# A hybrid SSM, RG-LRU, retention and RWKV-7 block: the order of issue of all engines taken from a list schedule of its own

## The chip, the cores and the metric

One Trainium2 chip, one of its cores. The metric is the device time of one execution in microseconds, the median of the runs. Engines: PE (TensorE, matmuls), PEld (its weight loads), DVE (VectorE), ACT (ScalarE), POOL (GpSimd), SP (SyncE, which issues most DMAs).

## What is computed

One layer over 512 tokens of width 1024, in float32. The normed input goes through one projection; four token mixers run in parallel on its parts; their outputs are projected, gated and summed; a convolutional feed-forward follows. Cut to its frame:

```python
def hybrid_mixer(h, w_in, ssm_p, lru_p, ret_p, rwkv_p, w_branch, w_out, cos, sin):
...
    proj = h @ w_in
...
    y_ssd = mamba2_branch(m_z, m_xbc, m_dt, *ssm_p)
    y_lru = rglru_branch(l_gate, l_x, *lru_p)
    y_ret = retention_branch(r_q, r_k, r_v, r_g, *ret_p, cos, sin)
    y_rwkv = rwkv7_branch(rw, *rwkv_p)
    ys = jnp.stack([y_ssd, y_lru, y_ret, y_rwkv], axis=2)
    branch = jnp.einsum('bsmw,mwd->bsmd', ys, w_branch)
    gates = jax.nn.sigmoid(gate_logits.astype(F32)).reshape(b, s, N_BRANCH, D_MODEL)
    merged = jnp.sum(gates * branch.astype(F32), axis=2).astype(h.dtype)
    return merged @ w_out
...
    u = causal_dwconv(h @ w_up, conv_w, conv_b)
    val, gt = jnp.split(u, 2, axis=-1)
    return (jax.nn.silu(gt) * val) @ w_down
...
        x = x + hybrid_mixer(h, w_in[l], ssm_p, lru_p, ret_p, rwkv_p, w_branch[l], w_out[l], cos, sin)
        h = rms_norm(x, norm_ffn[l])
        x = x + conv_ffn(h, ffn_up[l], ffn_conv_w[l], ffn_conv_b[l], ffn_down[l])
    return rms_norm(x, norm_final)
```

## The kernel before

Every projection works on tiles of 128 features by 512 tokens. A float32 product is made of three fp32r matmuls: `split` writes a rounded copy on ACT (L100: `whi`, `hh`, `yh`, `gh`) and the rest on DVE (L101: `wlo`, `hl`, ...), and `mm3` (L118) multiplies high by high, low by high and high by low into one of three PSUM tiles `acc` (L119, L120, L121). Weights come in blocks of 512 KB into `raw` (four buffers, `wraw`, L106). `proj_tokens` does the same with tokens on the partitions (L240 to L242), `tail_product` for the out and down products (L955 to L957). In this text a "product" is one such fp32r matmul.

The RWKV-7 mixer is a loop over eight pairs of heads (j = 0 to 7). `rwkv_a1` projects r, k and v and makes the decays; `rwkv_a2` makes the matrices of each chunk of 64 tokens (L372 on PE into `ra`), sends the 32x32 triangles through DRAM and solves them with 62 small DVE instructions (L426, L428); `rwkv_b` joins the inverses with 32 matmuls of 32x32 tiles (16 in L454, 16 in L464, into `rb`), copies on ACT between them (L458, L467), then goes through the eight chunks in sequence: L477 (PE), L479 (DVE), L481 (PE), L482 and L483 (ACT, DVE), L485 (PE), L488 (DVE). These matmuls, those of the other mixers (`inn`: L584, L664, L671, L673, L768, L798, L802, L812) and the transposes (L96) are in plain fp32 and short.

Between the parts of each j, `fill` (L914) takes steps of a generator: the lru tiles (`lru_tiles`: L585 sigmoid, L588 tanh, L591 exp, L598 sqrt, L602 gelu on ACT, each with a table of its own or shared), `ret_pair` and `mamba_group`, then `branch`, which projects the mixers' outputs and gates. After the eight pairs come the last branch, the out product, the up projection with its convolution (L1008, L1010) and the down product.

This is the order in which the code is recorded. The order in which each engine issues is made afterwards by the layer that records the program: it sorts the instructions of all engines by the recorded place and by a cost table that belongs to it, within the dependencies and the buffers. The code intervenes once: `with tc.issue_after(normed)` (L858) puts the setups of the lru and mamba mixers behind the last instruction of the norm. An engine takes its instructions in the order that was made, and waits where one isn't ready.

Of the kernel before, what the change touches and what calls it, by code (L numbers as in the profile page):

```python
# [9 lines left out]
F32R = mybir.dt.float32r  # L10
# [5 lines left out]
P = 128  # L16
# [29 lines left out]
for _key in ([("lora", 0), ("lora", 1)]  # L46
# [11 lines left out]
             + [("down", _j) for _j in range(22)]):  # L58
    _BLK[_key] = len(_BLK)
NBLK = len(_BLK)  # L60


@with_exitstack
def tile_hybrid_block(ctx, tc, x, wts, wzdt, lora, lruw, cpack, consts, rettab, nfin, out):
    nc = tc.nc
# [13 lines left out]
    def cols(name):  # L79
        o, n = _OFF[name]  # L80
        return cp[:, o:o + n]
# [7 lines left out]
    def cdram(name):  # L89
        o, n = _COFF[name]  # L90
        return consts[:, o:o + n]
# [54 lines left out]
    def rms_half(pool, psum, src, u, wname, hh, hl):  # L146

        ts = [src(2 * u + n) for n in range(2)]
        ss = pool.tile([P, 2], F32, name="nss", bufs=2)
        for n, t in enumerate(ts):  # L150
            sq = pool.tile([P, D], F32, name="nsq", bufs=1)
            nc.scalar.activation(out=sq, in_=t, func=AF.Square, accum_out=ss[:, n:n + 1])
        r = rsqrt_small(pool, ss, 1.0 / D, EPS, [P, 2], "nrs")
        xn = []
        for n, t in enumerate(ts):
            y = pool.tile([P, D], F32, name="nxn%d" % n, bufs=2)
            nc.vector.tensor_scalar(out=y, in0=t, scalar1=r[:, n:n + 1], scalar2=None, op0=ALU.mult)
            xn.append(y)
        w = slice(256 * u, 256 * u + 256)
        for ko in range(KT):  # L160
            ps = psum(ko)
            for n in range(2):
                transpose(ps[:, n * P:(n + 1) * P], xn[n][:, ko * P:(ko + 1) * P])
            nc.scalar.activation(out=hh[:, ko, w], in_=ps[:, 0:256], func=AF.Copy, scale=col(wname, ko))
            last = nc.vector.scalar_tensor_tensor(out=hl[:, ko, w], in0=ps[:, 0:256], scalar=col(wname, ko),
                                                  in1=hh[:, ko, w].bitcast(F32), op0=ALU.mult, op1=ALU.subtract)
        return last.ins
# [18 lines left out]
    acc = pss.enter_context(tc.tile_pool(name="acc", bufs=3, space=bass.MemoryType.PSUM))  # L186
    inn = pss.enter_context(tc.tile_pool(name="inn", bufs=1, space=bass.MemoryType.PSUM))
    rps = ExitStack()
    ra = rps.enter_context(tc.tile_pool(name="ra", bufs=2, space=bass.MemoryType.PSUM))
    rb = rps.enter_context(tc.tile_pool(name="rb", bufs=2, space=bass.MemoryType.PSUM))  # L190
    with tc.tile_pool(name="n1", bufs=1) as n1:
        xt, lw = [], []
        for i in range(NT):
            t = n1.tile([P, D], F32, name="x", bufs=4)
# [9 lines left out]
        for u in range(2):  # L204
            normed = rms_half(n1, lambda ko: pools[ko % 3].tile([P, S], F32, name=names[ko % 3]), lambda i: xt[i], u,
                              "norm_mix", hh, hl)
# [318 lines left out]
    def sm(shape):  # L525
        return fl.tile(shape, F32, name="sm", bufs=10)

    def bg(shape):
        return fl.tile(shape, F32, name="bg", bufs=6)
# [33 lines left out]
    def lru_setup():  # L563
        sp = softplus(fl, cols("lru_lam"), [P, 8], "lsp", neg=True)
        c8 = fl.tile([P, 8], F32, name="c8")
        nc.vector.tensor_scalar(out=c8, in0=sp, scalar1=8.0, scalar2=None, op0=ALU.mult)
        m8 = fl.tile([P, 8], F32, name="m8")
        nc.vector.tensor_scalar(out=m8, in0=sp, scalar1=-8.0, scalar2=None, op0=ALU.mult)
        return c8, m8
# [128 lines left out]
    def mamba_setup():  # L698
        z = fl.tile([P, NT, 16], F32, name="dtz")
        zt = bg([P, NT, 256])  # L700

        def put(i, ps):
            nc.vector.tensor_tensor(out=z[:, i, :], in0=ps[:, 256:272], in1=cols("dt_bias"), op=ALU.add)
            nc.scalar.activation(out=zt[:, i, :], in_=ps[:, 0:256], func=AF.Silu)
        proj_tokens("zdt", 0, put)
        dt = softplus(fl, z, [P, NT, 16], "dts")
        na = fl.tile([P, 16], F32, name="na")
        nc.scalar.activation(out=na, in_=cols("a_log"), func=AF.Exp)
        da = fl.tile([P, NT, 16], F32, name="da")
        nc.vector.scalar_tensor_tensor(out=da, in0=dt, scalar=-1.0, in1=na.unsqueeze(1).broadcast_to([P, NT, 16]),  # L710
                                       op0=ALU.mult, op1=ALU.mult)
        ps = inn.tile([P, S], F32, name="inn")
        daf = da.rearrange("p i h -> p (i h)")
        uo = sm([P, 2, P])
        for n, name in enumerate(("upper", "ones")):
            nc.sync.dma_start(out=uo[:, n], in_=cdram(name))
            nc.tensor.matmul(ps[:, n * 64:(n + 1) * 64], uo[:, n], daf, start=True, stop=True)
        ac = fl.tile([P, NT, 16], F32, name="acum")
        nc.vector.tensor_copy(out=ac, in_=ps[:, 0:64].rearrange("p (i h) -> p i h", h=16))
        cd = fl.tile([P, NT, 16], F32, name="cdec")  # L720
        nc.vector.tensor_copy(out=cd, in_=ps[:, 64:128].rearrange("p (i h) -> p i h", h=16))
        de = fl.tile([P, NT, 16], F32, name="dend")
        nc.vector.tensor_tensor(out=de, in0=cd, in1=ac, op=ALU.subtract)
        nc.scalar.activation(out=de, in_=de, func=AF.Exp)
        nc.scalar.activation(out=cd, in_=cd, func=AF.Exp)
        ea = fl.tile([P, NT, 16], F32, name="eac")
        nc.scalar.activation(out=ea, in_=ac, func=AF.Exp)
        ps = inn.tile([P, S], F32, name="inn")
        for i in range(NT):
            transpose(ps[0:16, i * P:(i + 1) * P], ac[:, i, :])  # L730
        at = sm([16, S])
        nc.scalar.copy(out=at, in_=ps[0:16])
        ad = dr.tile([16, S], F32, name="acd")
        nc.sync.dma_start(out=ad, in_=at)
        nac = fl.tile([P, NT, 16], F32, name="nac")
        nc.vector.tensor_scalar(out=nac, in0=ac, scalar1=-1.0, scalar2=None, op0=ALU.mult)
        cap = fl.tile([P, P], F32, name="cap")
        nc.sync.dma_start(out=cap, in_=cdram("cap"))
        return dt, nac, cd, de, ea, ad, cap, zt
# [115 lines left out]
    rope = []  # L855
    omu, hka, hwa, ones2r = rwkv_setup()
    lora_x = rwkv_lora()
    with tc.issue_after(normed):  # L858
        lru_c = lru_setup()
        mam = mamba_setup()  # L860
    msq = fl.tile([P, NT, 4], F32, name="msq")
    ym = dr.tile([NT, 4, P, 256], F32, name="ym")
    brs, mps = ExitStack(), ExitStack()
# [55 lines left out]
    for j in range(8):  # L919
        held = rwkv_a2(j, prep)  # L920
# [10 lines left out]
    tacc = pss.enter_context(tc.tile_pool(name="tacc", bufs=4, space=bass.MemoryType.PSUM))  # L931
# [54 lines left out]
    with ExitStack() as ff:  # L986
        with ExitStack() as up:
# [7 lines left out]
            for f in range(NFF):  # L995
                cv2 = []
                for n, j in enumerate((f, NFF + f)):
                    if first:
                        ps = first.pop(0)
                    else:  # L1000
                        wh, wl = wblock("up", j)
                        ps = tacc.tile([P, S], F32, name="acc")
                        for ko in range(KT):
                            s = slice(ko * P, (ko + 1) * P)
                            mm3(ps, wh[:, s], wl[:, s], hh[:, ko, :], hl[:, ko, :], ko == 0, ko == KT - 1)
                    t = cpool.tile([P, S], F32, name="fc%d" % n, bufs=2)
                    o = j * 3
# [9 lines left out]
        with ExitStack() as dn:  # L1017
# [5 lines left out]
            for dh in range(2):  # L1023
# [18 lines left out]
                    nc.scalar.dma_start(out=out[i * P:(i + 1) * P, S:], in_=ot[:, S:])  # L1042
                tail_product("down", NFF // 2, dh, gh, gl, add_y)
    pss.close()

# [44 lines left out]
def _layout(inputs):  # L1092
# [5 lines left out]
    m_z, m_xbc, m_dt, l_g, l_x, r_q, r_k, r_v, r_g, rw, gates = [int(v) for v in starts]  # L1098
    blocks = np.empty((NBLK, P, 1024), np.float32)

# [81 lines left out]
```

## Time and profile before

| | |
|---|---|
| median of 3 runs | 1602.02 us (1601.81 to 1602.98) |
| the profiled execution: its time, its span | 1603.08 us, 1601.3 us |
| PE busy | 1550.0 us (97%), 8324 matmul records |
| DVE, ACT, POOL busy | 1069.7 (67%), 722.5 (45%), 58.9 (4%) |
| chain that ended last | PE 75%, DVE 16%, ACT 5%, issue 3% |
| HBM traffic | 104 GB/s over the span |

PE's records are modelled at their ends and overlap, so what PE does is read from the starts. A 128x512 product is recorded with 0.39 us, while the next one starts earlier. Idle time of an engine in the listing by group stands behind the last bar, with the releaser.

### The profile page before, as it was taken

To read this page: it belongs to the slowest core of one execution; us is meant where nothing else is said; L and a number is where in the kernel's file an instruction comes from. 1 tells how busy PE (TensorE), PEld (TensorE's weight loads), DVE (VectorE), ACT (ScalarE), POOL (GpSimd) and SP (SyncE) were. 2 spreads that over 40 slices of the span, in tenths; PEclk is the share of its full clock that TensorE was granted. 3 is DMA by queue.
4 is the path that set the end of the run, shared out by engine and by line. 5 is a ranking of instruction groups with operands and counts; after the bars stand their busy time and mean duration, and the time that the engine had idled before them with its cause. 6 is when DMAs were issued, how large, how long until landed. Compare 5 with 4: busy or idle time off the path is not lost.

```text
span 1601.3 us, 22110 instructions
## 1 busy us (share of the span) xinstructions
PE 1550.0 (97%) x8324; PEld 1290.0 (81%) x8324; DVE 1069.7 (67%) x2334; ACT 722.5 (45%) x1190; POOL 58.9 (4%) x78
## 2 busy tenths in 40 slices
PE   7999989999999999999999999999999999999998
PEld 7788767877888788877788788888888888888886
DVE  6797788886887887897656857644436656555233
ACT  6463375535753576358323432323324444444123
POOL 1000000000000000000000100000000000000000
PEclk9999999999999999999999999999999999999999
DMA  5232132333243233443433333343222232233221
GB/s 206 93 125 77 70 115 77 100 107 86 93 126 98 78 112 83 126 132 115 163 105 100 112 104 108 116 151 136 101 79 93 96 104 93 96 101 107 101 96 53
DMA packets 108459, 169.44 MB, mean 106 GB/s; under 512 B 54832, under 2 KB 64304, under 8 KB 108352
## 3 DMA queue, kind: packets, MB, share of 16 engines
q1 hardware_dynamic: 107632, 166.92, 32.6%
q8 instruction: 65, 1.06, 0.3%
q10 hardware_dynamic: 720, 1.11, 0.2%
q14 instruction: 42, 0.34, 0.1%
HBM read 150.66 MB, written 15.24 MB: 104 GB/s over the span
## 4 chain that ended last, share of the span: by engine, by line
PE 75%; DVE 16%; ACT 5%; issue 3%; DMA 1%; SPq 0%; DVEq 0%; ACTq 0%
PE acc L119 16%; PE acc L120 16%; PE acc L121 16%; PE acc L955 3%; PE acc L957 3%; PE acc L956 3%; DVE wlo L101 2%; PE acc L240 2%; PE acc L242 2%; PE acc L241 2%; PE rb L477 2%; DVE prod L426 1%; DVE xr L428 1%; PE ra L372 1%; PE rb L485 1%
## 5 line engine op out<-in xcount | busy, mean ns | idle before, releaser
L119 PE MATMUL acc<-hh,whi 128*128 128x512 f32 (+1 forms) x1240 | 487.1, 393 | 7.1 <-ACT sm L602 4.7
L120 PE MATMUL acc<-hh,wlo 128*128 128x512 f32 (+1 forms) x1240 | 486.3, 392 | 1.0 <-DVE wlo L101 1.0
L121 PE MATMUL acc<-hl,whi 128*128 128x512 f32 (+1 forms) x1240 | 486.7, 393 | 0.0
L101 DVE TENSOR_TENSOR wlo<-raw,whi 128x1024 fp32r<-128x1024 f32 x228 | 279.1, 1225 | 163.2 <-ACT whi L100 162.4
L100 ACT CAST whi<-raw 128x1024 fp32r<-128x1024 f32 x228 | 237.9, 1045 | 214.7 <-PE acc L957 86.5
L119 PEld LDWEIGHTS acc<-hh,whi 128*128 128x128 f32 x1240 | 235.1, 190 | 51.5 <-ACT sm L602 5.4
L120 PEld LDWEIGHTS acc<-hh,wlo 128*128 128x128 f32 x1240 | 234.8, 189 | 44.4 <-DVE wlo L101 1.6
L121 PEld LDWEIGHTS acc<-hl,whi 128*128 128x128 f32 x1240 | 235.0, 190 | 43.5 <-issue 1.9
L1010 DVE SCALAR_TENSOR_TENSOR fc<-acc,fw,fc 128x511 f32<-128x511 f32 x88 | 65.9, 749 | 76.5 <-ACT fc L1008 74.9
L119 PE MATMUL acc<-yh,whi 128*128 128x512 f32 x256 | 101.7, 397 | 1.1 <-ACT yh L100 1.1
L121 PE MATMUL acc<-yl,whi 128*128 128x512 f32 x256 | 101.2, 395 | 0.2 <-DVE yl L101 0.2
L120 PE MATMUL acc<-yh,wlo 128*128 128x512 f32 x256 | 100.6, 393 | 0.0
L1008 ACT ACTIVATE fc<-acc,fw 128x512 f32<-128x512 f32 x44 | 34.3, 779 | 93.8 <-PE acc L121 93.8
L240 PE MATMUL acc<-whi,hh 128*128 128x256 f32 (+1 forms) x256 | 75.7, 296 | 0.4 <-ACT whi L100 0.4
L241 PE MATMUL acc<-wlo,hh 128*128 128x256 f32 (+1 forms) x256 | 74.2, 290 | 0.0
L242 PE MATMUL acc<-whi,hl 128*128 128x256 f32 (+1 forms) x256 | 74.1, 290 | 0.0
L955 PE MATMUL acc<-whi,gh 128*128 128x512 f32 x176 | 69.4, 395 | 0.0
L957 PE MATMUL acc<-whi,gl 128*128 128x512 f32 x176 | 69.4, 395 | 0.0
L956 PE MATMUL acc<-wlo,gh 128*128 128x512 f32 x176 | 69.4, 395 | 0.0
L884 ACT ACTIVATE gt<-acc 128x512 f32<-128x512 f32 x32 | 19.1, 598 | 88.1 <-PE acc L121 83.7
L426 DVE TENSOR_TENSOR prod<-nt,xr 128x60 f32<-128x60 f32 (+24 forms) x248 | 54.0, 218 | 5.2
L428 DVE TENSOR_TENSOR xr<-xr,prod 128x60 f32<-128x60 f32 (+24 forms) x248 | 53.8, 217 | 5.4
(331 smaller groups left out, 2369.1 us busy)
## 6 DMA issues: line engine op xcount, KB each, us to landing
raw<-in_wts_dram SPq DMA_DIRECT2D x226, 512.0 KB, 3.2
yr<-y SPq DMA_DIRECT2D x32, 256.0 KB, 3.0
y<-sm SPq DMA_DIRECT2D x24, 256.0 KB, 2.1
nt<-nd SPq DMA_DIRECT2D x32, 128.0 KB, 2.7
sm<-acd SPq DMA_DIRECT2D x16, 256.0 KB, 3.8
x<-in_x_dram SPq DMA_DIRECT2D x4, 512.0 KB, 5.3
sm<-sm SPq DMA_DIRECT2D x32, 64.0 KB, 2.0
ym<-bg SPq DMA_DIRECT2D x16, 128.0 KB, 1.7
```

The costliest lines, as they stand in the source:

```text
L100: nc.scalar.copy(out=hi, in_=src)
L101: nc.vector.tensor_tensor(out=lo, in0=src, in1=hi.bitcast(F32), op=ALU.subtract)
L119: nc.tensor.matmul(ps, wh, xh, start=first, stop=False)
L120: nc.tensor.matmul(ps, wl, xh, start=False, stop=False)
L121: nc.tensor.matmul(ps, wh, xl, start=False, stop=last)
L240: nc.tensor.matmul(o, hh[:, ko, t], wh[:, s], start=ko == 0, stop=False)
L241: nc.tensor.matmul(o, hh[:, ko, t], wl[:, s], start=False, stop=False)
L242: nc.tensor.matmul(o, hl[:, ko, t], wh[:, s], start=False, stop=ko == KT - 1)
L426: nc.vector.tensor_tensor(out=pr[:, 0:n, 0:m], in0=nt[:, jj, jj + 1:32].unsqueeze(2).broadcast_to([P, n, m]), in1=xr[:, jj:jj + 1, 0:m].br ...
L955: nc.tensor.matmul(ps[i], xh[:, ko, t], w[0][:, s], start=ko == 0, stop=False)
L956: nc.tensor.matmul(ps[i], xh[:, ko, t], w[1][:, s], start=False, stop=False)
L957: nc.tensor.matmul(ps[i], xl[:, ko, t], w[0][:, s], start=False, stop=ko == 2 * nblk - 1)
```

## The change

No instruction of the computation is touched. A function `_order` runs after the whole kernel is recorded. It works out what each instruction depends on by the overlap of what it reads and writes (for PSUM by the whole tile), what buffers it needs, and what it takes (`_cost`). Then it plans: the engine that is free first takes, among its ready instructions, the one recorded first; on PE, matmuls into `acc` come after all others, and any other matmul is left aside while its estimated start lies less than 150 ns back. At the end every instruction is tied behind the one planned before it on its engine, so that the layer's own sorting has no choice left. The one `issue_after` goes. All lines move by 261: L454 is L715 after, L464 is L725, L477 is L738, L119 to L121 are L380 to L382, L602 is L863.

```diff
+_MARGIN = 150.0
+_HOP = 60.0
...
+def _region(ap):
...
+    if t.space == bass.MemoryType.PSUM:
+        return 0, P, 1
...
+def _cost(i):
...
+    if kind == "InstMatmult":
+        mov, sta = i.ins[0].bass_ap, i.ins[1].bass_ap
+        if _base(out.tensor.name) == "acc" or mov.dtype == F32R:
+            return 13.5 + n / 2.4, 170.0
+        if i.is_transpose:
+            return 109.0, 170.0
+        if mov.shape[0] <= 32:
+            return 40.0, 170.0
+        return 2 * max(107.0, n / 1.2 + 2.5), 170.0
+    if kind == "InstDMACopy":
+        return 450.0, 0.0
...
+    return 158.0 + n * 1.04, _HOP
...
+def _order(tc, nc):
...
+                for o, w, q0, q1, b in lst:
+                    if (write or w or bank) and o != k and q0 < p1 and p0 < q1 and b & m:
+                        preds[k].add(o)
...
+        short[k] = i.engine == E.PE and o != "acc"
+        rank[k] = 1 if i.engine == E.PE and o == "acc" else 0
...
+        early = []
+        while ready[e] and short[ready[e][0][1]] and est[ready[e][0][1]] + _MARGIN > t:
+            early.append(heapq.heappop(ready[e]))
+        if early and not ready[e]:
+            heapq.heapify(early)
+            ready[e], early = early, []
+        k = heapq.heappop(ready[e])[1]
+        for x in early:
+            heapq.heappush(ready[e], x)
...
+            est[s] = max(est[s], t if k in after[s] else t + dur if ins[s].engine == e and e != E.SP else done[k])
...
+    for seq in order.values():
+        for a, b in zip(seq, seq[1:]):
+            tc.add_manual_dep(ins[b], ins[a].name, behind, reason="order of issue")
...
-    with tc.issue_after(normed):
-        lru_c = lru_setup()
-        mam = mamba_setup()
+    lru_c = lru_setup()
+    mam = mamba_setup()
...
+    _order(tc, nc)
```

PE at the first matmuls that join the inverses (`xr`, `ab`) for j = 1, before: one matmul, three products, the other fifteen in one piece.

```order
L119 MATMUL acc<-hh,whi 128x512
L454 MATMUL rb<-xr,ab 32x32
L120 MATMUL acc<-hh,wlo 128x512
L121 MATMUL acc<-hl,whi 128x512
L119 MATMUL acc<-hh,whi 128x512
L454 MATMUL rb<-xr,ab 32x32 x15
L120 MATMUL acc<-hh,wlo 128x512
```

After, at the same place, they alternate with the products one by one, up to the sixteenth.

```order
L380 MATMUL acc<-hh,whi 128x512
L715 MATMUL rb<-xr,ab 32x32
L381 MATMUL acc<-hh,wlo 128x512
L715 MATMUL rb<-xr,ab 32x32
L382 MATMUL acc<-hl,whi 128x512
L715 MATMUL rb<-xr,ab 32x32
L380 MATMUL acc<-hh,whi 128x512
L715 MATMUL rb<-xr,ab 32x32
```

Each of L454's matmuls (L715 now) has a product on either side. The second group (`tt`, `xr`) with the first matmuls of the chunks (`sv`, `g`), before: one of the sixteen, two of L477, products, then fifteen.

```order
L464 MATMUL rb<-tt,xr 32x32
L477 MATMUL rb<-sv,g 128x64 x2
L120 MATMUL acc<-hh,wlo 128x512
L121 MATMUL acc<-hl,whi 128x512
L119 MATMUL acc<-hh,whi 128x512
L120 MATMUL acc<-hh,wlo 128x512
L121 MATMUL acc<-hl,whi 128x512
L464 MATMUL rb<-tt,xr 32x32 x15
```

After, L464 (L725) and L477 (L738) stand between each other and between single products.

```order
L725 MATMUL rb<-tt,xr 32x32
L380 MATMUL acc<-hh,whi 128x512
L725 MATMUL rb<-tt,xr 32x32
L738 MATMUL rb<-sv,g 128x64
L725 MATMUL rb<-tt,xr 32x32
L381 MATMUL acc<-hh,wlo 128x512
L725 MATMUL rb<-tt,xr 32x32
L738 MATMUL rb<-sv,g 128x64
L725 MATMUL rb<-tt,xr 32x32
L382 MATMUL acc<-hl,whi 128x512
```

No piece is left there. ACT at the gelus of the first two lru tiles (`sm` from `acc`), before: a table load ahead of the sqrt, the exp and the gelu in turn.

```order
L598 ACT_TABLE_LOAD
L598 ACTIVATE sm<-sm 128x512
L591 ACT_TABLE_LOAD
L591 ACTIVATE sm<-sm,m_440 128x512
L602 ACT_TABLE_LOAD
L602 ACTIVATE sm<-acc 128x512
L593 ACTIVATE sm<-sm 128x512
L100 CAST lh_2399<-cs 128x256
L263 ACTIVATE pr<-acc,omu 128x512
L100 CAST whi<-raw 128x1024
L598 ACT_TABLE_LOAD
L598 ACTIVATE sm<-sm 128x512
```

After, the two sqrts stand together and so do the gelus, with one load each.

```order
L849 ACTIVATE sm<-sm,c_438 128x512
L852 ACT_TABLE_LOAD
L852 ACTIVATE sm<-sm,m_440 128x512
L854 ACTIVATE sm<-sm 128x512
L859 ACT_TABLE_LOAD
L859 ACTIVATE sm<-sm 128x512 x2
L524 ACTIVATE pr<-acc,omu 128x512
L863 ACT_TABLE_LOAD
L863 ACTIVATE sm<-acc 128x512
L361 CAST whi<-raw 128x1024
L863 ACTIVATE sm<-acc 128x512
```

The order after reaches the first gelu without an exp and its table between.

## Rows read from the trace of the kernel before

**Rows 1.** The page's first part: busy time, share of the span, instructions.

```profile
PE 1550.0 (97%) x8324; PEld 1290.0 (81%) x8324; DVE 1069.7 (67%) x2334; ACT 722.5 (45%) x1190; POOL 58.9 (4%) x78
```

**Rows 2.** PE's timeline, three stretches: start, busy us, line, tile, shape, count, idle before.

```profile
10.06 0.48 PE L96 MATMUL inn<-ident,nxn 128*128 128x128 f32 x1 [10.06 <-DVE nxn L157]
...
18.92 0.28 PE L119 MATMUL acc<-hh,whi 128*128 128x256 f32 x1
...
19.88 0.28 PE L121 MATMUL acc<-hl,whi 128*128 128x256 f32 x1
...
1592.32 0.40 PE L957 MATMUL acc<-whi,gl 128*128 128x512 f32 x1
...
1594.42 0.40 PE L957 MATMUL acc<-whi,gl 128*128 128x512 f32 x1
```

**Rows 3.** PE's timeline around L454 for j = 1.

```profile
254.85 0.39 PE L119 MATMUL acc<-hh,whi 128*128 128x512 f32 x1
...
255.53 0.39 PE L119 MATMUL acc<-hh,whi 128*128 128x512 f32 x1
255.85 0.28 PE L454 MATMUL rb<-xr,ab 32*32 32x32 f32 x2
...
256.39 0.39 PE L121 MATMUL acc<-hl,whi 128*128 128x512 f32 x1
256.62 0.40 PE L119 MATMUL acc<-hh,whi 128*128 128x512 f32 x1
256.95 1.09 PE L454 MATMUL rb<-xr,ab 32*32 32x32 f32 x30
...
258.30 0.39 PE L121 MATMUL acc<-hl,whi 128*128 128x512 f32 x1
```

**Rows 4.** Groups by shape, PE: count | busy us, mean ns | idle before, releaser.

```profile
L119 PE MATMUL acc<-hh,whi 128*128 128x512 f32 x1160 | 463.9, 400 | 7.1 <-ACT sm L602 4.7 <-ACT sm L689 2.4
...
L955 PE MATMUL acc<-whi,gh 128*128 128x512 f32 x176 | 69.4, 395 | 0.0
...
L240 PE MATMUL acc<-whi,hh 128*128 128x256 f32 x224 | 66.4, 297 | 0.0
```

**Rows 5.** PE's timeline at 128-row fp32 matmuls, alternating and in a piece.

```profile
161.00 0.40 PE L121 MATMUL acc<-hl,whi 128*128 128x512 f32 x1
161.23 0.33 PE L477 MATMUL rb<-sv,g 128*128 128x64 f32 x2
...
162.15 0.39 PE L121 MATMUL acc<-hl,whi 128*128 128x512 f32 x1
...
339.02 0.39 PE L121 MATMUL acc<-hl,whi 128*128 128x512 f32 x1
339.25 1.05 PE L664 MATMUL inn<-bg,sm 128*128 128x128 f32 x8
...
340.38 0.39 PE L120 MATMUL acc<-hh,wlo 128*128 128x512 f32 x1
```

**Rows 6.** Busy time by stretch: PE, PEld, DVE, ACT, POOL, granted clock, DMA share, GB/s.

```profile
226.40:229.70 3.30, 3.30 (x10) 2.53 (x9) 3.20 (x11) 3.27 (x5) 0.00 (x0) 0.50 0.21 79
```

**Rows 7.** Waits of PE: us in total, times, longest us.

```profile
PE acc L119 <- ACT sm L602: 4.7, 1, 4.7
```

**Rows 8.** PE's timeline around L464 for j = 2.

```profile
374.38 0.24 PE L464 MATMUL rb<-tt,xr 32*32 32x32 f32 x2
374.55 0.50 PE L119 MATMUL acc<-hh,whi 128*128 128x512 f32 x1
374.98 0.69 PE L464 MATMUL rb<-tt,xr 32*32 32x32 f32 x30
375.60 0.66 PE L477 MATMUL rb<-sv,g 128*128 128x64 f32 x4
```

**Rows 9.** Groups by shape, DVE.

```profile
L357 DVE SCALAR_TENSOR_TENSOR bk<-pa,di 64x512 f32<-64x512 f32 x16 | 19.2, 1203 | 3.4 <-ACT di L342 3.3
```

**Rows 10.** Timeline of the weight loads at the lone 32x32 matmul.

```profile
255.85 0.13 PEld L454 LDWEIGHTS rb<-xr,ab 32*32 32x32 f32 x2 [0.35 <-issue]
```

More of the change, by code (lines that the diff above doesn't have):

```diff
@@ L60, with _base, _elems @@
 NBLK = len(_BLK)
+_TABLES = {"Exp": ("exp",), "Tanh": ("exp", "sigmoid", "gelu", "silu"), "Sigmoid": ("sigmoid",), "Sqrt": ("sqrt",),
+           "Gelu_apprx_tanh": ("gelu",), "Silu": ("silu",)}
+_POOL_BUFS = {"acc": 3, "ra": 2, "rb": 2, "tacc": 4}
+_MARGIN = 150.0
+_HOP = 60.0
+def _base(name):
+    return name.rsplit("_", 1)[0]
+def _elems(ap):
+    n = 1
+    for x in ap.shape[1:]:
+        n *= x
+    return n
+_regions = {}
+def _region(ap):
+    t = ap.tensor
+    pitch = 1
+    for n in t.shape[1:]:
+        pitch *= n
+    if t.space == bass.MemoryType.PSUM:
+        return 0, P, 1
+    a = [(int(x[0]), int(x[1])) for x in ap.ap]
+    if t.space == bass.MemoryType.DRAM:
+        p0, n, off, rest = 0, 1, ap.offset, a
+    else:
+        p0, n, off, rest = ap.offset // pitch, a[0][1], ap.offset % pitch, a[1:]
+    key = (off, tuple(x for x in rest if x[0] and x[1] > 1))
+    m = _regions.get(key)
+    if m is None:
+        m = 1
+        for step, count in sorted(key[1]):
+            k = 1
+            while k < count:
+                d = min(k, count - k)
+                m |= m << (step * d)
+                k += d
+        m <<= off
+        _regions[key] = m
+    return p0, p0 + n, m
@@ new lines, in _cost @@
+def _cost(i):
+    E = mybir.EngineType
+    kind = type(i).__name__
+    out = i.outs[0].bass_ap
+    n = _elems(out)
+    if kind == "InstMatmult":
[9 more added lines that the diff above has]
+        return 450.0, 0.0
+    if i.engine == E.Activation:
+        extra = 0.0
+        if kind == "InstActivation":
+            extra = 90.0 * min(2, sum(1 for a in i.ins[1:] if getattr(a, "bass_ap", None) is not None))
+            if len(i.outs) > 1:
+                extra += 200.0
+        return 150.0 + n * 0.877 + extra, _HOP
+    if i.engine == E.Pool:
+        return 250.0 + n * (0.9 if kind == "InstMemset" else 1.0 if kind == "InstTensorCopy" else 2.4), _HOP
+    if getattr(i, "is_tensor_tensor_scan", False):
+        n *= 2
+    if kind == "InstTensorReduce":
+        n = _elems(i.ins[0].bass_ap)
+    return 158.0 + n * 1.04, _HOP
```

151 lines of the change are left out of this document (added).

## Prediction

> **What bounds the kernel now.** I read the busy times first, then the first and the last matmul, then the groups by shape, then single stretches of PE's timeline. PE is busy for 1550.0 us, 97% of the span of 1601.3 [rows 1]; no other engine gets over two thirds. PE's first matmul starts at 10.06; its last starts at 1594.42 and ends near 1594.8 [rows 2]. So of 51.3 us in which PE idles, 10.1 lie ahead of the first matmul and 6.5 behind the last, and 34.7 in between. An order of issue can gain only what PE loses between 10.06 and 1594.42, which are 1584.4 us.
>
> How much is that? I count from below, with distances from start to start, since a matmul's busy time (0.39 us for 128x512) runs past the start of the next. Products of 128x512 start every 0.227 (0.68 for three, 254.85 to 255.53) [rows 3], in the down product every 0.233 (nine from 1592.32 to 1594.42), those of 128x256 every 0.120 (eight from 18.92 to 19.88) [rows 2]. With the counts by shape [rows 4], where the other two lines of each triple have the same count and the branch product adds 3 x 256 and the short halves 3 x 80: 3 x (1160 + 256) x 0.227 = 964; 3 x (176 + 64) x 0.233 = 168; 3 x (224 + 80) x 0.120 = 109; 168 others 31. The fp32 records on 128 rows are 1764: 1684 at 0.112 (eight of L664: 339.02 to 340.38, less two products, are 0.906) [rows 5] and 80 wider ones, 212 together. The 32x32 matmuls take 11.5 where they stand in one piece (below). Sum 1496; PE takes 1584.4, so **88 us are lost**. Of these, 34.7 are recorded idle time; 43 waits cost 0.16 more each, the part of the busy time that runs past the next start (7). Behind the longest waits TensorE's clock was at its lower level of 1.2 GHz, in six stretches of 3.4 to 6.8 us, 30.6 in all; one is 226.4 to 229.7 [rows 6], right behind the wait for L602 [rows 7]. Half the rate there costs some 12. Switches to 32x32 tiles cost 10 and those between other pieces 5 (below). The rest, some 19, is waits too short to be recorded.
>
> **The change part by part.** Instructions stay, but for table loads on ScalarE (66 become 60) and waits on semaphores. What moves is the order, and on PE above all how finely it alternates: over the whole order, the fp32 matmuls stand in 378 pieces between the fp32r products before, and in 847 after. The new code makes them so: a short matmul is taken only if its estimated start lies 150 ns back, and matmuls into one PSUM tile depend on each other, so the second of four becomes ready as the first ends. It is put off, and a long product goes between. The 32x32 matmuls of L454 and L464 (128 each) stand in 30 pieces before and in 236 after, 233 of them single.
>
> *32x32 matmuls, the large term.* One alone: from the product at 255.53 to the second one behind it at 256.39 are 0.86 us; less two products (0.454) it costs 0.406. Fifteen in one piece: 256.62 to 258.30 are 1.68, less 0.454 are 1.226 [rows 3]. From the two lengths a piece costs 0.348 and each matmul in it 0.058. L464: one matmul, one product and the next matmul take 374.38 to 374.98, 0.60; less 0.227 that is 0.373; the piece of fifteen behind it lasts 0.62 to the next matmul [rows 8], so it is 0.032 for each and 0.341 for a piece. The stretch at 374.38, matmul, product, matmul, is already what the new order writes everywhere. Where the neighbours are alike, all 30 pieces show these distances within 0.02 us. 206 more pieces at 0.348: **+71.7 us**, all of it on PE's own path.
>
> *128-row fp32 matmuls.* Their pieces go from some 360 to 681. Two matmuls of L477 that alternate with products cost 161.00 to 162.15 less three products, 0.469, so 0.235 each [rows 5], against 0.224 in one piece. 320 more pieces at 0.012: **+4 us**. Bounds are 0, and 16 if each lost 0.05.
>
> *Waits.* Of the 88 us, 15 are switches; 73 are waits and the slow clock behind them. How many stay can't be read from an order. For their going: 25 of the 34.7 recorded us are short matmuls that stood at PE's head before their operand was there, which is what the 150 ns are meant for; and PE will run behind the plan by those 72 us (the code takes 40 ns for a 32x32 matmul), so other engines are ahead of it. The longest, 4.7 us for L602 on ScalarE [rows 7], came from table loads in a row; the new order loads once for two gelus. Against it: the plan takes 158 + 1.04 n ns on VectorE, 690 for the L357 that feeds L372, and the trace has 1203 [rows 9]; semaphores of the DMA queue aren't in it at all. What is late next is VectorE's chain between L477 and L488 and the split of the weights (L101). Bounds: none stays (-73), all stay (0). I let a third stay, 24, since most of the plan's durations are the trace's and its misses are few: **-49 us**.
>
> *Clock in the alternating pieces.* Sixteen 32x32 matmuls now take about 10 us, in which products fill 0.227 of 0.60. At 1.2 GHz each product could take 0.2 more: 0 to 47 us for 236. No row shows such a stretch of 10 us; the nearest, at 374.38, ran at 2.4 GHz, and the clock fell behind idle time. I take a sixth, **+8 us**.
>
> Start and end: the first ten transposes, the loads of x and the rows behind the last product stand in both orders alike, so 10.1 and 6.5 us stay.
>
> [...] The weight load of the lone 32x32 matmul starts at 255.85, with its matmul, and its loader had idled for 0.35 us [rows 10]. [...]
>
> **Rivals.** (1) *The forecast*: 1603.1 + 71.7 + 4 - 49 + 8 = 1637.8. (2) *The plan doesn't hold on the chip*: it is tighter, every late operand stops PE, and all 73 us of waits stay or come back elsewhere: 1603.1 + 71.7 + 4 + 8 = 1687. L357 speaks for it, PE's lag against it. (3) *The plan holds exactly*: no wait is left, the clock stays up: 1603.1 + 75.7 - 73 = 1606, about no change. (4) *Not slower: the switch of tiles is hidden between products.* Its place is the 233 single matmuls; a separation would cost near 0 in place of 0.348, as if the loader ran ahead: 1637.8 - 71.7 = 1566, faster by 2%. It decides below 0.18 us for each of the 206 (71.7 less the 34.7 by which the forecast is slower, over 206). All 30 pieces and [rows 10] stand against it. (5) *The order isn't what runs*: excluded, as each engine takes the instructions of the built program in turn, and that program has the single matmuls.
>
> **How the numbers follow.** The sum stands against the profiled execution, 1603.08 us; the median of the runs is 1602.02, 1.06 lower, so 1637.8 becomes 1637. Chances: forecast 0.67 (waits and clock between 12 and 57 us in place of 32: 1616 to 1662), plan doesn't hold 0.15 (1662 to 1700), plan exact 0.10 (1600 to 1616, half of it within the bound of no change), hidden switch 0.08. Leaving out the last and most of the second's upper half gives 1608 to 1670. A measurement of this kernel tells about 0.2% from no change, 3.2 us, so slower begins at 1605.2: 0.67 + 0.15 + 0.05 = 0.87; no change 0.05; faster 0.08.
>
> **What would show it.** L715 and L725 (L454 and L464 before) keep their counts, but alternate with products, each product behind one lasting 0.50 and each of them starting 0.32 or more behind its neighbour. PE's busy share stays at 97% or rises while the span grows: the switch hides in busy time. PE's idle time between first and last matmul falls from 34.7 to 10 to 20 us, the 4.7 at the first L863 (L602 before) among what goes. Stretches with nothing but products, behind 1030 us of before, keep their length. Wrong would be the price, if a single 32x32 matmul costs under 0.2 us; the term of the waits, if the idle time stays near 35; the clock term, if 1.2 GHz holds through most of the alternating pieces.

## The result and the profile after

The changed kernel takes 1803.25 us, the median of 4 runs (1794.57 to 1806.22), against 1602.5 of the kernel before on the same chip: 1.125 times as long, with an interval from 1.122 to 1.127. I had forecast slower, but 1637, with 1670 as the upper end. So the sign came out as forecast and the size didn't: +201 us instead of +35.

The page of after, busy time by engine (answers to [rows 1]):

```profile
PE 1715.3 (95%) x8324; PEld 1377.0 (76%) x8324; DVE 1089.8 (60%) x2334; ACT 717.7 (40%) x1184; POOL 58.9 (3%) x78
```

PE has the same number of records and 165 us more busy time. Its idle time grew as well: the span is 1804.2, less 1715.3 that is 88.9; 10.4 lie ahead of the first matmul and 6.5 behind the last, which leaves 72.0 between first and last, where before had 34.7.

The first thing to look at is the granted clock. The core's span and its mean granted clock, before and after:

```profile
core 0: 1601.3 us, clock 0.990
core 0: 1804.2 us, clock 0.913
```

And by stretches of 200 us (columns as in [rows 6]: PE, PEld, DVE, ACT, POOL, granted clock, DMA share, GB/s):

```profile
200.00:400.00 200.00, 180.70 (x952) 143.12 (x951) 148.34 (x354) 90.57 (x161) 11.79 (x16) 0.87 0.26 77
...
1000.00:1200.00 200.00, 196.91 (x871) 144.76 (x871) 100.98 (x231) 54.82 (x91) 6.36 (x8) 0.85 0.25 76
1200.00:1400.00 200.00, 199.17 (x887) 163.96 (x886) 88.27 (x120) 58.34 (x76) 0.00 (x0) 1.00 0.36 123
```

In both traces the granted clock is recorded in stretches, each at 1.00 or at 0.50 (before 14, after 44 of them, the shortest 3.4 us), so a mean of 0.913 means 2 x 0.087 x 1804 = 314 us at 0.50; before, the mean was 0.990, 32 us. No trace shows the clock in GHz: where the prediction and the expectations write 2.4 and 1.2 GHz, the traces show 1.00 and 0.50, and the starts of products an estimated 2.4 and 1.2 columns per ns (at 1.00, 256 more columns take 0.227 less 0.120 us [rows 3] [rows 2]; at 0.50, six products of 512 start in 2.56 us, 226.64 to 229.20 of before). But for 3.4 us at 1434 and the end of the span, the low clock ends near 1175 us, where the last of the eight RWKV blocks ends; the down product runs as before (L1215, L955 before, has a mean of 395 ns in both).

PE's timeline after, at the sixteen matmuls of L715 (L454 before) for j = 7; start, busy us, line, tile, shape (answers to [rows 3]):

```profile
1141.19 0.50 PE L380 MATMUL acc<-yh,whi 128*128 128x512 f32 x1
1141.62 0.28 PE L715 MATMUL rb<-xr,ab 32*32 32x32 f32 x2
1141.83 0.50 PE L381 MATMUL acc<-yh,wlo 128*128 128x512 f32 x1
1142.26 0.28 PE L715 MATMUL rb<-xr,ab 32*32 32x32 f32 x2
...
1144.69 0.80 PE L382 MATMUL acc<-yl,whi 128*128 128x512 f32 x1
1145.42 0.31 PE L715 MATMUL rb<-xr,ab 32*32 32x32 f32 x2
1145.66 0.80 PE L380 MATMUL acc<-yh,whi 128*128 128x512 f32 x1
1146.38 0.31 PE L715 MATMUL rb<-xr,ab 32*32 32x32 f32 x2
```

Read the starts. Up to 1143 one product and one 32x32 matmul take 0.64 us; the forecast had 0.227 + 0.406 = 0.633. From 1144 on the same pair takes 0.96 to 0.97. Between them the clock fell, as busy time and granted clock of the stretches show (j = 7 ahead of the fall and behind it, then j = 6):

```profile
1140.30:1143.80 3.50, 3.50 (x19) 1.79 (x18) 0.00 (x0) 0.00 (x0) 0.00 (x0) 1.00 1.02 281
1143.80:1174.50 30.70, 30.70 (x96) 17.43 (x96) 3.45 (x7) 2.70 (x6) 0.00 (x0) 0.50 0.06 19
997.00:1031.20 34.20, 34.20 (x107) 18.21 (x106) 3.44 (x4) 4.03 (x7) 0.00 (x0) 0.50 0.10 35
```

PE's busy time equals the length of each stretch: no wait is recorded in them, and yet the clock stays at 0.50 for over 30 us, while the 32x32 matmuls come one by one. It recovers soon after they end. The last of j = 6 starts at 1027.85, from 1028.68 products alone start every 0.43 us, from 1031.22 every 0.23:

```profile
1027.85 0.31 PE L725 MATMUL rb<-tt,xr 32*32 32x32 f32 x2
...
1028.68 0.63 PE L381 MATMUL acc<-hh,wlo 128*128 128x512 f32 x1
1029.11 0.63 PE L382 MATMUL acc<-hl,whi 128*128 128x512 f32 x1
...
1031.22 0.39 PE L381 MATMUL acc<-hh,wlo 128*128 128x512 f32 x1
1031.45 0.40 PE L382 MATMUL acc<-hl,whi 128*128 128x512 f32 x1
```

Waits of PE after (us in total, times, longest; answers to [rows 7]):

```profile
PE rb L715 <- DMA xr<-xd: 12.9, 9, 2.8
PE inn L357 <- DVE nxn L418: 10.4, 1, 10.4
PE acc L380 <- DVE prod L687: 7.2, 2, 4.9
PE acc L380 <- ACT sm L863: 6.7, 1, 6.7
PE ra L357 <- DVE bk L642: 6.1, 3, 3.5
```

The second line is the start of the kernel. The wait for the first gelu, 4.7 us before, is 6.7; and the first 32x32 matmul of every block now waits for its DMA.

### The profile page after: what moved, and what is told of

The parts are those of the page before. It is cut to its first block, busy times and chain, and to the rows that moved or that the text cites. A ratio compares the mean times of both kernels' runs of the same rounds, so it can differ in the third digit from the quotient of the medians.

```text
span 1804.2 us, 22101 instructions
## 1 busy us (share of the span) xinstructions
PE 1715.3 (95%) x8324; PEld 1377.0 (76%) x8324; DVE 1089.8 (60%) x2334; ACT 717.7 (40%) x1184; POOL 58.9 (3%) x78
## 4 chain that ended last, share of the span: by engine, by line
PE 75%; DVE 13%; DMA 5%; ACT 3%; issue 2%; SPq 2%; POOL 0%; DVEq 0%; ACTq 0%; POOLq 0%
PE acc L381 16%; PE acc L380 16%; PE acc L382 15%; PE acc L1215 3%; PE acc L1217 3%; PE acc L1216 3%; PE acc L502 2%; PE acc L503 2%; PE acc L501 2%; PE rb L715 2%; PE rb L725 1%; DVE wlo L362 1%; DMA xr<-xd 1%; PE rb L738 1%; DVE sm L820 1%
## 5 line engine op out<-in xcount | busy, mean ns | idle before, releaser
L380 PE MATMUL acc<-hh,whi 128*128 128x512 f32 (+1 forms) x1240 | 514.5, 415 | 19.6 <-DVE prod L687 7.2
L381 PE MATMUL acc<-hh,wlo 128*128 128x512 f32 (+1 forms) x1240 | 514.2, 415 | 4.6 <-DVE wlo L362 4.6
L382 PE MATMUL acc<-hl,whi 128*128 128x512 f32 (+1 forms) x1240 | 513.2, 414 | 0.2
L380 PEld LDWEIGHTS acc<-hh,whi 128*128 128x128 f32 x1240 | 243.2, 196 | 68.8 <-issue 10.1
L381 PEld LDWEIGHTS acc<-hh,wlo 128*128 128x128 f32 x1240 | 243.1, 196 | 51.8 <-DVE wlo L362 6.5
L382 PEld LDWEIGHTS acc<-hl,whi 128*128 128x128 f32 x1240 | 242.5, 196 | 46.4 <-issue 2.3
L380 PE MATMUL acc<-yh,whi 128*128 128x512 f32 x256 | 107.0, 418 | 0.1
L382 PE MATMUL acc<-yl,whi 128*128 128x512 f32 x256 | 106.6, 417 | 0.0
L501 PE MATMUL acc<-whi,hh 128*128 128x256 f32 (+1 forms) x256 | 84.0, 330 | 3.7 <-DVE sm L820 2.8
L502 PE MATMUL acc<-wlo,hh 128*128 128x256 f32 (+1 forms) x256 | 84.4, 331 | 2.4 <-DVE wlo L362 2.4
L503 PE MATMUL acc<-whi,hl 128*128 128x256 f32 (+1 forms) x256 | 83.6, 328 | 0.0
L1215 PE MATMUL acc<-whi,gh 128*128 128x512 f32 x176 | 69.5, 395 | 0.0
L715 PEld LDWEIGHTS rb<-xr,ab 32*32 32x32 f32 x256 | 20.5, 127 | 54.9 <-issue 38.5
L501 PEld LDWEIGHTS acc<-whi,hh 128*128 128x128 f32 x256 | 54.9, 215 | 5.9 <-ACT whi L361 3.0
```

What stands on the lines that cost most here:

```text
L380: nc.tensor.matmul(ps, wh, xh, start=first, stop=False)
L381: nc.tensor.matmul(ps, wl, xh, start=False, stop=False)
L382: nc.tensor.matmul(ps, wh, xl, start=False, stop=last)
L501: nc.tensor.matmul(o, hh[:, ko, t], wh[:, s], start=ko == 0, stop=False)
L502: nc.tensor.matmul(o, hh[:, ko, t], wl[:, s], start=False, stop=False)
L503: nc.tensor.matmul(o, hl[:, ko, t], wh[:, s], start=False, stop=ko == KT - 1)
```

## The experiments

Two things had to be told apart: what the single 32x32 matmuls cost, with the clock (theory A: they alone bring it down; theory B: the new waits do, or the alternation of all short matmuls), and where the 72 us of idle time come from. A piece is a run of 32x32 matmuls with no other matmul between them. The ratios are to the kernel before as measured beside each run; clock and idle time are those of the profiled run. "Idle" below is PE's recorded idle time between its first and last matmul; "at 0.50" is worked out from the mean clock as above.

| kernel | median us | against before | 32x32 pieces | at 0.50, us | idle, us | idle in its plan, us |
|---|---|---|---|---|---|---|
| before | 1602.5 | 1 | 30 | 32 | 35 | |
| after | 1803.3 | 1.125 | 236 | 314 | 72 | 76 |
| e0_fixed | 1601.8 | 0.999 | 30 | 29 | 35 | |
| e1_group32 | 1648.5 | 1.030 | 31 | 82 | 71 | 76 |
| e2_spread | 1695.1 | 1.058 | 138 | 159 | 45 | |
| e3_grouptr | 1800.1 | 1.125 | 236 | 299 | 73 | 76 |
| e5_late | 1788.2 | 1.118 | 237 | 275 | 67 | 89 |
| e8_fours | 1672.7 | 1.044 | 76 | 114 | 72 | 76 |
| e6_margin0 | 1640.8 | 1.025 | 30 | 88 | 53 | 52 |
| e7_late0 | 1599.5 | 0.998 | 31 | 29 | 38 | 51 |
| e9_lead | 1583.1 | 0.988 | 29 | 41 | 24 | 32 |

The last column is no measurement: the list schedule gives every matmul a start while it plans, and the gaps between these are added up. The regrouped kernels (e1, e3, e8) keep the plan of after.

**The 32x32 matmuls put back together, nothing else.** The order of after on every engine; of each sixteen the first stays and fifteen move to the place of the last.

```diff
+    tied = {}
+    for k in order[E.PE]:
+        i = ins[k]
+        if i.ins[0].bass_ap.shape[0] <= 32:
+            tied.setdefault(i.outs[0].bass_ap.tensor.name, []).append(k)
+    moved = {k: g for g in tied.values() for k in g[1:]}
+    order[E.PE] = [x for k in order[E.PE] for x in ((k,) if k not in moved else moved[k][1:] if k == moved[k][-1] else ())]
```

> The changed kernel's order on every engine, but of each set of sixteen 32x32 matmuls the last fifteen stand together where the last of them stood (31 pieces of 32x32 work instead of 236; the alternation of all other short matmuls with products stays). Theory A (the 32x32 matmuls one by one between products cost the switch, and that alternation is also what holds the clock at 1.2 GHz): 205 pieces x 0.35 us at full clock plus some 64 us that the same pieces lost to the lower clock go, and some 15 us of other matmuls in those stretches: 1650 to 1670 us, and the stretches with a granted clock of 0.5 shrink from 312 us to under 130 us. Theory B (the lower clock comes from the new waits and from the alternation of all short matmuls, the 32x32 ones only pay the switch): 72 us go and no more, 1720 to 1740 us, with over 220 us at a granted clock of 0.5.

Measured: 1648.47 us, 155 less than after, ratio to before 1.030 (1.028 to 1.032). Its span and clock:

```profile
core 0: 1646.3 us, clock 0.975
```

Its timeline at the piece of fifteen for j = 7 (L722 is L715 of after):

```profile
1006.46 0.39 PE L387 MATMUL acc<-yh,whi 128*128 128x512 f32 x1
1006.78 1.09 PE L722 MATMUL rb<-xr,ab 32*32 32x32 f32 x30
1007.80 0.50 PE L388 MATMUL acc<-yh,wlo 128*128 128x512 f32 x1
```

The whole block of j = 7, busy time and granted clock:

```profile
1002.50:1013.50 11.00, 10.78 (x102) 8.35 (x103) 3.60 (x5) 1.84 (x4) 0.00 (x0) 1.00 0.45 116
```

The block that took some 30 us, nearly all at 0.50, takes 11 at 1.00, with the same 32 matmuls in it. 205 pieces fewer are worth 0.755 us each: 0.348 is the price of a piece from [rows 3], 71 us together, and the remaining 83 us are put down to the clock (314 to 82 us at 0.50). What one microsecond at 0.50 costs can be estimated from runs of one kernel that differ in it: after took 1794.57 us in the run with a clock of 0.922 (280 us at 0.50) and 1806.22 in one with 0.913 (314), about a third of a us for each. At that price 232 us fewer are worth some 78, near the 83. Theory A. What is left above before is 46 us.

**The 32x32 matmuls parted, in the order of before.** The order of before on all engines, written down as a table; a 32x32 matmul (`tiny`) that is followed by another takes one product from behind between them, where one stands ahead of the next matmul into a tile that isn't `rb` (`pe` is PE's order).

```diff
+    while pe:
+        out.append(pe.pop(0))
+        if tiny(out[-1]) and pe and tiny(pe[0]):
+            n = next(n for n, i in enumerate(pe) if product(i) or "rb" not in i.outs[0].bass_ap.tensor.name)
+            if product(pe[n]):
+                out.append(pe.pop(n))
```

> The order of the kernel before on every engine, but 32x32 matmuls that stood together are parted by one product each, taken from behind them (138 pieces of 32x32 work instead of 30; all else in the order of before). Theory A: 108 pieces x 0.35 us = 38 us for the switch, and the spread stretches run at 1.2 GHz, so that a piece costs near 0.66: 1665 to 1685 us, with stretches of granted clock 0.5 at the spread pieces and over 90 us in all (before: 34). Theory B: 38 us for the switch at full clock and no more, 1635 to 1645 us, the clock as before.

The table without any move is the control; both kernels tie the instructions in the same way:

```diff
+    order = {e: [ins["I-%d" % x] for x in _seq(s) if "I-%d" % x in ins] for e, s in _SEQ.items()}
...
+            tc.add_manual_dep(b, a.name, behind, reason="order of issue")
```

> The order of the kernel before on every engine, written down as a table and laid on the instructions in the way the changed kernel lays its own order; nothing is moved. Both theories: that an order is laid on at all costs nothing, 1598 to 1606 us, 30 to 40 us at a granted clock of 0.5. If tying every instruction to the one ahead of it had a price of its own, it would show here and in the kernel with the parted 32x32 matmuls alike: over 1620 us.

Measured: the control 1601.75 (0.998 to 1.000 of before), the parted kernel 1695.06, 93 us more. That is above both forecasts: 108 pieces at 0.348 are 38, 10 us are idle time (45 instead of 35, the chain behind the parted matmuls runs later), and the rest, some 45, goes with 159 us at 0.50, 130 more than the control's (some 43 at a third of a us each). Around the fall of the clock for j = 7 (L563 is L454 before):

```profile
1079.50 0.49 PE L229 MATMUL acc<-hh,wlo 128*128 128x512 f32 x1
1079.93 0.28 PE L563 MATMUL rb<-xr,ab 32*32 32x32 f32 x2
1080.13 0.79 PE L230 MATMUL acc<-hl,whi 128*128 128x512 f32 x1
1080.86 0.31 PE L563 MATMUL rb<-xr,ab 32*32 32x32 f32 x2
```

The pair goes from 0.63 to 0.97 us in the middle of the alternation. In the order of before, without the new plan, the clock falls at the parted 32x32 matmuls (159 us at 0.50, the control's 29). In five of the eight blocks no idle time at all is recorded between the first of them and the fall; in one, j = 5, the clock doesn't fall. Theory B fails.

**Other short matmuls put together.** As the first experiment, for the transposes: 91 pieces of 128-row work fewer, the 32x32 matmuls single.

```diff
-        if i.ins[0].bass_ap.shape[0] <= 32:
+        if i.is_transpose:
```

> The changed kernel's order, but transposes into one tile of PSUM stand together behind the first of them (91 pieces fewer of 128-row fp32 work); the 32x32 matmuls alternate with products as in the changed kernel. Theory A: the alternation of 128-row short matmuls costs next to nothing: 1790 to 1805 us, and as much time at a granted clock of 0.5 as the changed kernel has (312 us). Theory B: part of the alternation behind the lower clock goes: under 1780 us, with under 270 us at 0.5.

Measured 1800.14 (1799.21 to 1806.01), where after lies between 1794.57 and 1806.22: no difference. The alternation of the transposes costs nothing that can be seen. It can't be told here whether it is free: at the forecast's 0.012 us a piece, 91 pieces are 1 us, at its bound of 0.05 they are 5, and both lie within the spread.

**The waits for DMAs taken out, the 32x32 matmuls single.** In the plan, readers come 3.5 us instead of 1.5 us behind a DMA's packets.

```diff
-            done[k] = wire + 1500.0
+            done[k] = wire + 3500.0
```

> The changed kernel's own list schedule, but with 3.5 us instead of 1.5 us from the end of a DMA's packets to the moment its readers may be issued, so that the plan no longer puts the first 32x32 matmul ahead of its data (the wait of some 2 us in each of eight blocks); 32x32 matmuls alternate with products as in the changed kernel. Theory A: the waits for DMAs go (up to 25 us of 72), but the clock still falls in the alternating stretches, without a wait ahead of them: 1770 to 1800 us, over 220 us at a granted clock of 0.5. Theory B (the waits bring the clock down): the alternating stretches run at 2.4 GHz: 1690 to 1720 us.

Measured 1788.16. Of the waits for xr one is left, 1.2 us; the idle time is only 5 us less, since other waits grew. Here the clock can be seen to fall with no idle time ahead of it (stretches of j = 7, columns as above):

```profile
1129.00:1134.00 5.00, 5.00 (x25) 3.55 (x23) 0.90 (x1) 1.22 (x2) 0.00 (x0) 1.00 0.86 229
1134.00:1139.40 5.40, 5.40 (x26) 2.71 (x25) 1.23 (x1) 0.31 (x1) 0.00 (x0) 1.00 0.30 111
1139.40:1166.70 27.30, 27.30 (x86) 15.78 (x86) 3.41 (x7) 2.71 (x6) 0.00 (x0) 0.50 0.06 20
```

PE is busy for every microsecond of the three stretches. The single matmuls begin at 1132.90, the clock falls at 1139.4, and it stays down until 1166.7, 5.7 us behind the start of the last of them. The last idle time recorded ahead of this fall ends at 947.67, over 190 us earlier. In six of the eight blocks of this run the clock falls without any recorded idle time between the first 32x32 matmul and the fall. No wait stood ahead of these six falls.

**In fours.** As the first experiment, but each four stands together, with products between one four and the next.

```diff
-    moved = {k: g for g in tied.values() for k in g[1:]}
+    moved = {k: g[n:n + 4] for g in tied.values() for n in range(0, 16, 4) for k in g[max(n, 1):n + 4]}
...
```

> The changed kernel's order on every engine, but the 32x32 matmuls stand in fours, each four where the last of it stood, with three or four products between one four and the next (76 pieces of 32x32 work; singly 236, regrouped 31). If the switch costs 0.35 us and the clock falls only where switches are dense: 1648 + 45 x 0.35 = 1664 us, 83 to 110 us at a granted clock of 0.5. If any return to 32x32 work within some microseconds brings the clock down: half of the stretches at 0.5 stay, 1685 to 1710 us, with over 150 us at 0.5.

Measured 1672.66: 24 us above the regrouped kernel for 45 pieces, 0.54 each. 16 of the 24 are the switch at 0.348; the time at 0.50 is 114 us instead of 82, worth some 11 at a third of a us. Nearer the first expectation, if outside both: with a few products between two pieces the clock mostly held here (114 us at 0.50 of a span of 1671).

**What is left: 46 us over before, with 71 us of idle time.** The plan of after, added up, has 76 us of idle time on PE by itself, the first gelu with 7.2 us among it (on the chip 6.7). The next run sets the margin to zero; the one behind it has the later DMAs as well, as in e5.

```diff
-_MARGIN = 150.0
+_MARGIN = 0.0
...
-            done[k] = wire + 1500.0
+            done[k] = wire + 3500.0
```

> The changed kernel's list schedule with one number changed: a short matmul may be taken as soon as it is ready in the plan (margin 0 instead of 150 ns). The 32x32 matmuls then stand together (30 pieces, as before the change), and the 128-row short matmuls are less often alone (384 pieces of short work against 847 in the changed kernel and 700 in the regrouped one). The plan's own idle time of TensorE between its first and last matmul, added up while the plan is made, falls from 76 to 52 us. Theory A (the idle time that the changed kernel and the regrouped one show, 72 and 71 us, is in the plan itself): 24 us less than the regrouped kernel's 1648 and some 5 us for fewer pieces and less low clock: 1615 to 1630 us, with 48 to 58 us of idle time. Theory B (the waits come from what the plan doesn't know, as the landing of DMAs): idle time stays near 70 us, 1640 to 1650 us.

> As the kernel with margin 0, and the plan also counts 3.5 us instead of 1.5 us from a DMA's packets to its readers. The plan's own idle time is 51 us. Theory A: what is left of waits for DMAs (about 16 us in the regrouped kernel) goes, the rest is the plan's: 1600 to 1617 us, idle time 45 to 55 us. Theory B: the DMAs were most of the excess, idle time under 40 us: under 1595 us.

Measured 1640.82 with margin 0, and 1599.48 (0.998 of before, 0.997 to 1.000) with the later DMAs as well. In the first the idle time is 53 us, 18 under the regrouped kernel's and as the first theory has it (52 planned); yet the time is only 8 us lower, which is the second theory's range. The match of 52 and 53 is in part chance. The largest sum of waits on the chip is one that the plan doesn't have, since this plan puts no idle time ahead of any 32x32 matmul:

```profile
PE rb L715 <- DMA xr<-xd: 13.1, 7, 3.2
```

With the matmuls of plan and trace put side by side, by the number of products ahead of them, some 31 of the 53 us lie where the plan has idle time too, and some 21 us of the plan's aren't recorded. Of the missing gain, a part is the clock: by the granted clock of each run, this kernel has 88 to 105 us at 0.50, the regrouped one 76 to 89. The rest isn't settled.

What stands behind one of these waits, in stretches around it for j = 7 (columns as above):

```profile
981.00:985.20 4.20, 2.56 (x13) 1.74 (x11) 2.52 (x3) 1.05 (x1) 0.00 (x0) 1.00 0.74 174
985.30:995.50 10.20, 10.20 (x85) 7.66 (x84) 0.52 (x2) 1.66 (x5) 0.00 (x0) 0.50 0.15 50
995.50:1000.00 4.50, 4.50 (x24) 3.81 (x24) 2.17 (x5) 1.63 (x3) 0.00 (x0) 1.00 0.01 2
```

A wait of 1.64 us ends at 984.60, and 10.2 us at 0.50 follow. Not every wait has this behind it: of the seven, four are followed by such a stretch within 3 us (3.4, 10.2, 6.8 and 10.2 us long, 30.6 together) and three aren't; in the regrouped kernel five waits for xr last 1.5 to 2.5 us, and only one has a stretch behind it, of 3.4 us. The block of that kernel shown above, at 1.00 throughout, begins as a wait of 1.48 us ends.

The run with later DMAs waits for xr once, 0.3 us; it has 38 us of idle time (15 less) and 29 us at 0.50 instead of 88. It is 41 us faster. Of these, 15 are idle time, and the 59 us at 0.50 are worth some 20 by the estimate above; about half of these 59 stood behind waits for xr. The rest fell away with a plan that differs in more than these waits, and isn't told apart. So the later landing in the plan gave more than the 16 us I expected of it: the time stays at the edge of the first theory, the idle time is in the second's range. Of the 38 us some 31 lie where the plan has idle time, and some 20 of the planned aren't recorded; why, was not tried. 3.5 us is more than the DMA of xr takes from issue to landing (DMA issues of after: KB each, median us to landing):

```profile
xr<-xd SPq DMA_DIRECT2D x16, 32.0 KB, 2.7
```

**A plan with less idle time.** If the plan's idle time tells of the chip's, the plan can be improved by itself. With margin 0 and the later DMAs kept, the order of preference is shifted for 17 kinds of results, found by trying shifts for the least planned idle time.

```diff
+_LEAD = {"DVE rst": 200, "DVE rrsu": 100, "Activation cs": 200, "PE inn": -200, "DVE wlo": 50, "DVE ab": -200,
+         "DVE st": -800, "Activation xr": -200, "Activation nsq": -400, "Activation bt": -200, "DVE dtz": 100,
+         "PE ra": -100, "DVE mss": 1600, "Activation pk": 400, "Activation pr": -800, "DVE nxn0": -100, "DVE cs": 100}
...
+        key[k] = k - _LEAD.get(str(i.engine).split(".")[-1] + " " + o, 0)
...
-            heapq.heappush(ready[e], (rank[k], k))
+            heapq.heappush(ready[e], (rank[k], key[k], k))
```

> As the kernel with margin 0 and 3.5 us for DMAs, and the plan's order of preference (program order) is shifted for 17 kinds of results, so many places earlier or later, found by trying shifts on the plan alone for the least planned idle time: 32 us instead of 51 us between TensorE's first and last matmul, 29 pieces of 32x32 work. Theory A (idle time on the chip follows the plan's, and with short waits the clock stays at 2.4 GHz): 20 us under the kernel with 3.5 us and margin 0 and some 5 us for the clock: 1578 to 1595 us, below the kernel before. Theory B (the chip departs from a tighter plan and gives the gain back in other waits): 1600 us or more.

Measured 1583.09 us, 0.988 of before (0.986 to 0.991): 1.2% under before, with an interval that excludes 1, and less than any other kernel here. Its busy times:

```profile
PE 1541.4 (97%) x8324; PEld 1293.7 (82%) x8324; DVE 1085.4 (69%) x2334; ACT 711.1 (45%) x1181; POOL 59.5 (4%) x78
```

Its largest waits:

```profile
PE rb L359 <- DVE nxn L420: 11.0, 1, 11.0
PE inn L1061 <- DVE sm L1047: 7.8, 4, 3.4
PE acc L382 <- ACT sm L865: 5.2, 1, 5.2
```

Idle 1582.9 - 1541.4 - 11.0 - 6.5 = 24 us, 32 in the plan. The first line is the start of the kernel; the wait for the first gelu (L865 here) is 5.2 us, the longest single one behind the start.

## Why the prediction missed

**What held.** PE is the bound, and an order can change only what lies between its first and last matmul: 10.4 and 6.5 us outside them stayed. The price of a lone 32x32 matmul at a granted clock of 1.00 held (0.64 us for the pair, forecast 0.633), so the term of +72 stands; the 71 of the first experiment are this price times 205 and no second measurement. The rival by which the switch hides, which no row had shown, is out; the weight loads of these matmuls idle with no other releaser than issue, as in [rows 10], 193 times for 256 matmuls (total, times, longest):

```profile
PEld rb L715 <- issue: 38.5, 108, 0.7
PEld rb L725 <- issue: 32.4, 85, 0.7
```

What PE does in the 0.35 us a piece isn't shown by the trace. The term of the 128-row matmuls (+4) isn't contradicted: e3 moved 91 of their pieces and no time that can be seen.

**The step "Clock in the alternating pieces": forecast +8, bounds 0 to 47; measured some 83** (the remainder of the first experiment; some 78 by the price of the time at 0.50). Both the value and the upper bound failed. I bounded the loss by the product alone, 0.2 us for each of 236, and took a sixth, since the one row of this kind, 374.38 [rows 8], ran at 1.00 and every fall of the clock before stood behind idle time (six falls, idle times of 0.36 to 4.68 us). But that row is a single pair; nothing before showed ten in a row, and a neighbour that far away can't carry a small value. On the chip a pair loses 0.33 us, 236 of them up to 78, and the other products in these blocks slow down too (0.43 us from start to start at 1028.68, 0.23 at 1031.22). Here stretches with no recorded idle time ran at 0.50 (30.70 of 30.70 us busy from 1143.80 on), so PE's recorded busy share didn't tell whether the clock held.

**The step "Waits": forecast -49, measured about +46 with the clock behind them.** The sign failed. I asked whether the plan holds on the chip, and took a plan that holds for one without waits. Added up, it has 76 us of idle time itself, a number that the code could have told before any run, and the chip has 72. The two sums are near each other, but not the same waits throughout: some 51 of the 72 us lie where the plan has them, the first gelu among them (7.2 planned, 6.7 measured); the 12.9 us for xr aren't in the plan, and some 24 us of the plan's aren't recorded. Two numbers in the plan make up the +46: the 150 ns, which I read as removing waits, put short matmuls off and cost 24 us of planned idle time and 8 us on the chip; and the 1.5 us for DMAs, 41 us with the clock. I had noted that semaphores of the DMA queue aren't in the plan, and gave them no price. My reading of ScalarE at the first gelu failed with it. There is one table load for two gelus, but the loads ahead of the first one are as many as before: five in the 13 us up to it after, and five in the last 12 us before (at 213.89, 215.93, 220.01, 221.95 and 223.98 in the trace of before). After (start, us, line):

```profile
240.64 1.28 ACT L852 ACT_TABLE_LOAD   x1
...
242.68 1.28 ACT L846 ACT_TABLE_LOAD   x1
...
246.76 1.28 ACT L852 ACT_TABLE_LOAD   x1
...
249.45 1.28 ACT L859 ACT_TABLE_LOAD   x1
...
252.49 1.28 ACT L863 ACT_TABLE_LOAD   x1
```

**The sum.** 72 (as forecast) + 83 instead of 8 + 46 instead of -49 are 201. It closes by its making: 83 is what the first experiment took away beyond the price of the pieces, 46 is what it left. Whatever the 128-row matmuls cost is in the 46. Slower came out because the switch term held. The second rival (1687, all waits stay) came nearest, and a part of its reason holds, the waits that the plan doesn't know; the larger part of the waits is in the plan. The range failed since neither bound was wide enough: with 0 for the waits and 47 for the clock the sum would have been 1725, still 78 short. I had let no wait be added, and the clock cost nothing but the products between.

**The signs I had named.** L715 and L725 alternate with products of 0.50, as said. PE's share fell to 95% instead of staying at 97; idle time is 72 instead of 10 to 20; the wait of 4.7 grew to 6.7; and the granted clock is 0.50 through most of the alternating pieces (314 us in all), which I had put down as the mark of a wrong clock term. The stretches with nothing but products keep their length, as said: the down product takes 122.2 us from its first start to its last in both kernels.

## What to carry to other kernels

A schedule that counts matmuls by their own durations must also know what stands beside them: here small tiles belonged together, since each return to them cost 0.348 us, and alternating with them cost the clock of everything around (0.50 for 30.70 us at j = 7 of after, some 83 us in all). When an order comes from a plan, add up the plan's own idle time on the bounding engine before asking whether the chip will follow it; the best kernel (1583 us) came from lowering that number. Then look whether the waits on the chip are those of the plan: where the sums agree (52 and 53 in e6), they can still be different waits, and here the ones for DMAs came on top. A wait on PE can have a stretch at the slow clock behind it (in e6 1.64 us had 10.2 us at 0.50, and four of seven waits for xr had one), and should be counted with that: from e6 to e7, 15 us of idle time went with 41 us of the time.

## What the runs showed of the hardware

TensorE's granted clock fell to 0.50 without a recorded idle gap, in a stretch of single 32x32 matmuls between 128x512 products (e5: busy 27.30 of 27.30 us from 1139.40 on, the last recorded idle time ahead of it over 190 us back), and stayed there until 5.7 us behind the start of the last of them. The same 32 matmuls, fifteen of each sixteen in one piece, ran at 1.00 (e1, 1002.5 to 1013.5), with the other short matmuls alternating as before; where they were parted in the order of before, the clock fell again (e2, 159 us at 0.50 against 29). A lone 32x32 matmul between products cost 0.35 us more than one in a piece at a granted clock of 1.00 (0.406 and 0.058 [rows 3]). What in the alternation brought the clock down, the small tile or the 0.35 us that each lone one cost, is open: no run had one without the other.
